# Later scalings of queries and keys, and one more tile for raw weights, in a two-layer decoder trunk

## The chip, the cores and the metric

The kernel runs on one core of one Trainium2 chip. The metric is the device time of one execution in microseconds (us), lower is better. The engines have short names here: PE is TensorE (matmuls), DVE is VectorE, ACT is ScalarE, POOL is GpSimd, and SP is SyncE, which here only issues DMA transfers. POOL also issues some.

## The reference

Two layers act on x of 512 tokens by 2048 features, all in float32. Layer 0 is forgetting attention (FoX) with 16 heads of 128, layer 1 multi-scale retention with 8 heads (queries and keys of 256, values of 512). Each mixer's output is multiplied by a SiLU gate before the output projection. What matters here, cut to its core:

```python
# layer 0
q, k, v, gate, f_logit = split(x @ fox_w_in)           # 2048 columns each, 16 for f_logit
q = rms_norm(q, q_gain); k = rms_norm(k, k_gain)       # per head: x * rsqrt(mean(x^2) + eps) * gain
c = cumsum(log_sigmoid(f_logit + b_f))
p = softmax(q @ k.T * 128**-0.5 + c_i - c_j, causal)
h = layer_norm(sqrt(2) * x + (p @ v * silu(gate)) @ fox_w_out)
# layer 1
q, k, v, gate = split(h @ ret_w_in)                    # 2048, 2048, 4096, 4096 columns
o = retention(rotary(q), rotary(k), v)                 # decay per head
out = layer_norm(sqrt(2) * h + (group_norm(o) * silu(gate)) @ ret_w_out)
```

`sqrt(2)` is `DEEPNORM_ALPHA` for a depth of 2.

## The kernel before

**Products.** Every float32 matrix is split into a high part (ACT copies it to a reduced float32, L340) and a low part (DVE subtracts the high part, L341); a product is three matmuls, high by high, low by high and high by low (`mm3`, L345 to L347). The projections are done in units. A unit multiplies a 2048 by 1024 (wide) or 2048 by 512 (narrow) slice of weights by a Strassen-Winograd scheme: seven products, called p1 to p7, instead of eight, with sums of quarters of the weights and of the activations. A product is cut into blocks: four in a wide unit, two in a narrow one. A wide block is twelve matmuls of 512 columns.

**Weights of a block.** A quarter of the weights comes by DMA on SP's queue into a raw tile, `w_raw` (L615); the first quarter goes into `w_q` (L606), a running sum. DVE adds a raw tile to `w_q` (L635) or two raw tiles to one another (L630), then ACT and DVE split the sum into `w_h` and `w_l`. There are three raw tiles, st0 to st2. `new_raw` takes the tile that has been free longest from a list called `stock`, and `end_raw` puts it back. The products p3 and p7 together need two raw tiles per block.

**Order of the work.** The order of all instructions is written out when the program is built, by a planner (class `Order`). Time is counted in slots, one for each block of matmuls. In a slot the planner first finishes the block before, adds weights three blocks ahead and splits two ahead, loads up to nine ahead as long as raw tiles are free, writes the block's matmuls, and then lets side tasks take steps. A side task is a generator: `yield need(dve=..., wait=n)` asks that n slots have passed since its last step, that named tiles are free, and that the work put on DVE (and on ACT) since does not exceed an allowance, 4.4 us for DVE, of which each slot works off 2.72. When a block needs a tile that is not free, the planner writes rounds of 2.7 us without matmuls until the tasks have freed it (`require`).

**Queries and keys of layer 0.** The heads are treated in eight pairs. A unit's sinks copy a pair's raw queries and keys into the tiles in0 and in1 (L1088) while ACT sums their squares (L1113). For every second pair (2 and 4) the copy is parked in DRAM and fetched later. The task `normed` then makes the reciprocal roots: DVE writes a first guess by integer arithmetic (L313 to L315), and three rounds of Newton's method follow. In pairs 6 and 7 (`quick`) DVE does these too; in pairs 0 to 5 POOL does, four small operations a round (L333 to L336, `iterate_aside`). After a wait in slots the four scalings follow on DVE (L1177), then PE transposes the scaled rows (L1209), and ACT and DVE split them by L1188 and L1190. With that in0 and in1 are free for the next pair, and the two heads of the pair, tasks of their own, can go on to scores, softmax and the product with the values.

**The last units.** Units 14 to 17 are the second output projection, all wide. Unit 16 adds the residual to the first half of the columns, and unit 17 to the second half, in the tiles g0, g2 and in0 with in1 (`add_z`, L1594, with the statistics for the layer norm at L1605). L517 and L525 finish the sums of products of a unit and free their PSUM banks. Meanwhile other forms of the activations are fetched (L949) and split for the second half of the units' sum.

**Lending.** The task `lend` takes a tile that has no user for some time, puts it into `stock` as one more raw tile, and takes it out again when a flag is set and the tile is back in `stock`. Before, it is used once, for the tile k0 in the first unit. Another such tile, `room`, is lent by `split_room` and given back by `join_room` when unit 16 begins.

Of the kernel before, what the change touches and what calls it, by code (L numbers as in the profile page):

```python
# [53 lines left out]
FIRST = (("p2",), ("p1",))  # L54
REST = (("p5",), ("p6",), ("p3", "p7"), ("p4",))
# [35 lines left out]
class Order:  # L91
# [21 lines left out]
    def give(self, ring, after=0):  # L113
        if after:
            self.later.append((self.now + after, ring))
        elif ring == "mmp" and not self.soon(self.due):

            self.emptied.append(self.due)
        else:
            self.free[ring] += 1  # L120
# [15 lines left out]
    def spawn(self, steps, rank=2):  # L136

        task = dict(steps=steps, last=self.now - 1, rank=rank)
        try:
            task["need"] = next(steps)  # L140
        except StopIteration:
            return
        at = sum(t["rank"] <= rank for t in self.tasks)
        self.tasks.insert(at, task)
# [103 lines left out]
def need(dve=0.0, act=0.0, pe=0.0, wait=1, until=lambda: True, **rings):  # L248
    return dict(dve=dve, act=act, pe=pe, wait=wait, until=until, rings=rings)
# [3 lines left out]
def trunk(ctx: ExitStack, tc: tile.TileContext, xq, x, fb_f, columns, wf_in, narrow, wide, ln_g, ln_b, rot, decay,  # L253
# [7 lines left out]
    spawn, take, give, free, require = o.spawn, o.take, o.give, o.free, o.require  # L261

    def f32(t):
        return t.bitcast(F32)

    def sb8(name, tag, dt=F32):
        return pool.tile([P, 4, 512], dt, name=name, tag=tag)
# [36 lines left out]
    def rsqrt(*args):  # L304
        for _ in rsqrt_steps(*args, steps=False):
            pass

    def rsqrt_steps(dst, src, n, scale, eps, aside=None, steps=True):

        h = pool.tile([P, n], F32, name="rsq_h", tag=f"rsq_h{n}")  # L310
        t = pool.tile([P, n], F32, name="rsq_t", tag=f"rsq_t{n}")

        nc.vector.tensor_scalar(h, src, 0.5 * scale, 0.5 * eps, op0=ALU.mult, op1=ALU.add)  # L313
        nc.vector.tensor_scalar(t.bitcast(I32), h.bitcast(I32), 1, None, op0=ALU.logical_shift_right)
        nc.vector.tensor_scalar(dst.bitcast(I32), t.bitcast(I32), -1.0, float(0x5EF759DF - 2 ** 31),  # L315
                                op0=ALU.mult, op1=ALU.add)
        if aside is not None:
            aside.append((h, t, dst))
            return
        for i in range(3):  # L320
            if i == 1 and steps:
                yield need(dve=1.2, wait=0)
            if n == 1:
                nc.vector.scalar_tensor_tensor(t, dst, h, dst, op0=ALU.mult, op1=ALU.mult)
            else:
                nc.vector.tensor_mul(t, dst, dst)
                nc.vector.tensor_mul(t, t, h)
            nc.vector.scalar_tensor_tensor(dst, t, 1.5, dst, op0=ALU.subtract, op1=ALU.mult)

    def iterate_aside(h, t, r):  # L330

        for _ in range(3):
            nc.gpsimd.tensor_mul(t, r, r)  # L333
            nc.gpsimd.tensor_mul(t, t, h)
            nc.gpsimd.tensor_scalar(t, t, -1.5, None, op0=ALU.add)
            nc.gpsimd.tensor_mul(r, r, t)  # L336
# [26 lines left out]
    stock, whose = ["st0", "st1", "st2"], {}  # L363
# [14 lines left out]
        take("y0")  # L378
        give("g2")

    def lend(tag):

        yield need(**{tag: 1})
        take(tag)
        stock.append(tag)
        give("st")
        yield need(until=lambda: fox.get("wide") and tag in stock and free["st"])
        stock.remove(tag)
        take("st")
        give(tag)  # L390
# [614 lines left out]
    fox = dict(heads=0, norms=0, emptied=0)  # L1005
# [62 lines left out]
    class Pair:  # L1068
# [13 lines left out]
        def take(self, m, n, tile, done):  # L1082
            def copy():
                yield need(act=0.5, until=self.has_room)
                if self.raw is None:
                    self.new_raw()
                    self.new_sums()
                nc.scalar.activation(self.raw[m][:, :, n * 256:(n + 1) * 256], tile, AF.Copy)  # L1088
                yield need(act=1.2)
                self.squares(m, n, tile, 0)  # L1090
                done()
                self.have += 1

            spawn(copy(), 0)
# [62 lines left out]
        def normed(self):  # L1157

            yield need(until=lambda: self.have == 4 and fox["norms"] == self.i)
            raw = [self.raw[s // 2][:, s % 2] for s in range(ST)]  # L1160
            r = self.ss
            flat = [r.rearrange("p a b -> p (a b)")] * 2
            if self.quick:
                yield need(dve=1.2)
                yield from rsqrt_steps(*flat, 4 * ST, 1.0 / P, QK_EPS)
            else:
                yield need(dve=0.6)
                guess = []
                rsqrt(*flat, 4 * ST, 1.0 / P, QK_EPS, guess)
                iterate_aside(*guess[0])  # L1170
                yield need(wait=2)
            scaled = {}
            for s in range(ST):
                yield need(dve=0.6, wait=0)
                scaled[s] = o.due
                v = raw[s].rearrange("p (h d) -> p h d", h=4)
                nc.vector.tensor_mul(v, v, r[:, s, :, None].to_broadcast([P, 4, P]))  # L1177
            yield need(until=lambda: all(free[t] for t in self.tags))
            for t in self.tags:
                take(t)  # L1180
            self.qk = sb8("qk_h", self.tags[0], F32R), sb8("qk_l", self.tags[1], F32R)

            def to_parts(t, s):

                parts = [(gain, t[:, i:i + 2], *(p[:, i:i + 2, s * P:(s + 1) * P] for p in self.qk))
                         for i, gain in ((0, gq), (2, gk))]
                for gain, x, h, _ in parts:
                    nc.scalar.activation(h, x, AF.Copy, scale=gain)  # L1188
                for gain, x, h, l in parts:
                    nc.vector.scalar_tensor_tensor(l, x, gain, f32(h), op0=ALU.mult, op1=ALU.subtract)  # L1190
                self.due = o.due
                give("mmp")

            t, s, last = {}, ST if self.quick else 0, None
            for q in range(ST if self.quick else 0):
                yield need(act=0.75, dve=0.7, pe=0.45, wait=1 - q % 2, mmp=1, until=lambda: o.soon(scaled[q]))
                t[q] = by4(mmp())
                for h in range(4):
                    nc.tensor.transpose(t[q][:, h], raw[q][:, h * P:(h + 1) * P], ident)
                to_parts(t[q], q)  # L1200
            can = lambda: s < ST and free["mmp"] and o.soon(scaled[s])
            while s < ST or last is not None:
                yield need(act=0.75, dve=0.7, pe=0.45, until=lambda: last is not None or can())
                new = None
                if can():
                    new = s
                    t[s] = by4(mmp())
                    for h in range(4):
                        nc.tensor.transpose(t[s][:, h], raw[s][:, h * P:(h + 1) * P], ident)  # L1209
                    s += 1  # L1210
                if last is not None:
                    to_parts(t[last], last)
                last = new
            give("in0")
            give("in1")
            fox["emptied"] = self.i + 1
            yield need()
            fox["norms"] = self.i + 1
# [232 lines left out]
    vg = [Unit(wide, g, gate_and_value(g), u2="k2") for g in range(4)]  # L1451
# [19 lines left out]
            else:  # L1471
                halves[i] = partial(split_x, *part)
    first.run(BOTH, halves=halves, then={len(BOTH) - 1: lambda: (spawn(forget()), core(0))}, before=before, ahead=ahead)
    vg[0].run(FIRST + REST, then={"p1": lambda: spawn(lend("k0")), "p7": lambda: fox.update(wide=True)})
    for i in (1, 3):
        both[i].run(then={"p4": lambda i=i: (core(i), spawn(pairs[i + 1].fetch()), core(i + 1))})
        vg[(i + 1) // 2].run()
# [44 lines left out]
    def two_banks():  # L1522
# [5 lines left out]
        BOTH, then={len(BOTH) // 2 - 1: lambda: spawn(fetch("a21", "k2", "k0", "k1")), len(BOTH) - 1: late})  # L1528
# [3 lines left out]
    st = {}  # L1532
# [182 lines left out]
    def last_banks():  # L1715
# [4 lines left out]
    sink, steps = add_z(0, ALPHA, x_rows, "plain", 2)  # L1720
    Plain(wide, 4, sink, last_banks).run(
        HELD, then={8: lambda s=steps: spawn(s(), 1)})
# [6 lines left out]
    sink, steps = add_z(1, ALPHA, x_rows, "each")  # L1729
# [256 lines left out]
    for h in heads[1:]:  # L1986
        if h.h == 2:
            spawn(biases())
        h.qk_unit.run(then={"p3": lambda h=h: spawn(h.attend())})
        then = fetch_while(1) if h.h == RH - 1 else {}  # L1990
        last = then.get("p4", lambda: None)
        h.vg_unit.run(SLOW if h.h == 1 else ORDER, leaves=h.h == RH - 1,
                      then={**then, "p4": lambda h=h, last=last: (spawn(h.retain()), last())})
# [106 lines left out]
    half = lambda s, c: z_res[s, c]  # L2100
    spawn(join_room(), 0)
    sink, steps = add_z(0, 1, half, "order")
    Unit(wide, 16, sink, u2="k2").run(then={0: lambda s=steps: spawn(s(), 1)})
    sink, steps = add_z(1, 1, half, "early")
    Unit(wide, 17, sink, u2="k2").run(EARLY, then={0: lambda s=steps: (spawn(s(), 1), spawn(biases_there(), 0)), "p2": lambda: spawn(last_gains(), 0),
                                          "p3": lambda: (spawn(first_stores(), 0), spawn(last_stores()))}, last=True)
# [53 lines left out]
```

## Time and profile before

| | us |
|---|---|
| median of 3 runs | 2323.4 |
| lowest and highest run | 2322.31, 2323.48 |
| the profiled execution | 2324.2 |
| its span, from the first to the last instruction | 2322.4 |

The profile is one execution, recorded by the hardware profiler. Its page gives busy times, a chain of waits, groups of instructions and DMA issues; the trace behind it can be asked for waits, for the instructions in order of time, and for sums over windows. A row of the timeline reads: start, duration, engine, line, operation, output <- inputs, shapes, count of merged instructions, and in brackets the idle time of the engine just before it and what ended that. A row of waits reads: engine, line and output that waited, what it waited for, and the total, the number and the longest of the waits. Matmuls are pipelined: a matmul's row lasts longer than the distance to the next start, so PE's speed is read from starts.

### The profile page before, as it was taken

The numbers are of one execution on the slowest core, as the hardware profiler recorded it, in microseconds if no ns is written. First come the engines' busy times: TensorE is split into PE (matmuls) and PEld (weight loads), VectorE is DVE, ScalarE is ACT, GpSimd is POOL, SyncE is SP. The second block draws the span as 40 slices with busy tenths as digits, with TensorE's granted clock in tenths as the row PEclk, the third lists the DMA queues.
The fourth block names the chain that finished last, engine by engine and source line by source line (L and its number), as shares of the span: only waits on it lengthen the run. The fifth ranks groups of instructions, "written<-read, shape, count | busy, mean of one in ns | idle before, by whom it ended". The sixth has DMA issues, their size and how long they took to land.

```text
span 2322.4 us, 32788 instructions
## 1 busy us (share of the span) xinstructions
PE 2288.3 (99%) x12381; PEld 1969.6 (85%) x12381; DVE 1869.8 (81%) x2375; ACT 1219.0 (52%) x1795; POOL 200.6 (9%) x323
## 2 busy tenths in 40 slices
PE   9999999999999999999999999999999999999996
PEld 9888788788899888889889898988888898788785
DVE  5886787787765666789989888888988889988888
ACT  4555656556555535664544445354545445555534
POOL 0100110111000000010101001010101001020001
PEclk9999999999999999999999999999999999999998
DMA  6465465454545467784675757575656658698767
GB/s 230 144 211 189 167 197 185 168 191 157 197 156 162 137 215 241 244 215 157 213 254 207 235 180 228 194 203 196 212 183 198 210 173 268 206 252 276 240 219 205
DMA packets 162687, 471.07 MB, mean 203 GB/s; under 512 B 17472, under 2 KB 34000, under 8 KB 162016
## 3 DMA queue, kind: packets, MB, share of 16 engines
q1 hardware_dynamic: 136464, 395.02, 50.1%
q0 software_dynamic: 26064, 73.95, 13.0%
q8 instruction: 97, 1.59, 0.3%
q14 instruction: 62, 0.51, 0.1%
HBM read 409.10 MB, written 64.00 MB: 204 GB/s over the span
## 4 chain that ended last, share of the span: by engine, by line
PE 85%; DVE 7%; ACT 3%; issue 2%; DMA 2%; POOL 1%; SPq 0%; DVEq 0%; ACTq 0%; POOLq 0%
PE acc L345 25%; PE acc L346 25%; PE acc L347 25%; DVE w_l L341 3%; PE mmp L345 2%; PE mmp L346 2%; PE mmp L347 2%; ACT w_h L340 2%; DVE w_q L635 2%; PE mmp L1390 1%; DMA w_raw<-in_wide 1%; PE mmp L1242 1%; DMA room<-in_wide 1%; PE mmp L1941 1%; PE mmp L1209 0%
## 5 line engine op out<-in xcount | busy, mean ns | idle before, releaser
L340 ACT ACTIVATE w_h<-w_q 128x1024 fp32r<-128x1024 f32 x360 | 380.9, 1059 | 436.8 <-DVE w_q L635 229.1
L345 PE MATMUL acc<-w_h,a 128*128 128x512 f32 (+1 forms) x1440 | 534.3, 371 | 3.3 <-DVE kept L525 2.5
L341 DVE TENSOR_TENSOR w_l<-w_raw,w_h 128x1024 fp32r<-128x1024 f32 (+1 forms) x311 | 379.2, 1219 | 189.3 <-ACT w_h L340 187.8
L346 PE MATMUL acc<-w_l,a 128*128 128x512 f32 (+1 forms) x1440 | 527.2, 366 | 1.9 <-DVE w_l L341 1.9
L340 ACT ACTIVATE w_h<-w_raw 128x1024 fp32r<-128x1024 f32 (+1 forms) x311 | 328.3, 1056 | 379.6 <-PE acc L347 186.7
L347 PE MATMUL acc<-w_h,a 128*128 128x512 f32 (+1 forms) x1440 | 527.5, 366 | 0.0
L341 DVE TENSOR_TENSOR w_l<-w_q,w_h 128x1024 fp32r<-128x1024 f32 x360 | 439.7, 1222 | 108.0 <-ACT w_h L340 101.0
L346 PE MATMUL acc<-w_l,s 128*128 128x512 f32 (+1 forms) x1280 | 487.3, 381 | 8.2 <-DVE w_l L341 8.2
L345 PE MATMUL acc<-w_h,s 128*128 128x512 f32 (+1 forms) x1280 | 491.9, 384 | 0.0
L347 PE MATMUL acc<-w_h,s 128*128 128x512 f32 (+1 forms) x1280 | 486.3, 380 | 0.0
L345 PEld LDWEIGHTS acc<-w_h,a 128*128 128x128 f32 x1440 | 271.7, 189 | 48.1 <-issue 5.9
L346 PEld LDWEIGHTS acc<-w_l,a 128*128 128x128 f32 x1440 | 271.9, 189 | 45.0 <-DVE w_l L341 4.0
L347 PEld LDWEIGHTS acc<-w_h,a 128*128 128x128 f32 x1440 | 271.5, 189 | 45.0
L346 PEld LDWEIGHTS acc<-w_l,s 128*128 128x128 f32 x1280 | 241.6, 189 | 55.3 <-DVE w_l L341 13.4
L347 PEld LDWEIGHTS acc<-w_h,s 128*128 128x128 f32 x1280 | 241.2, 188 | 46.1
L345 PEld LDWEIGHTS acc<-w_h,s 128*128 128x128 f32 x1280 | 241.3, 189 | 43.2 <-issue 0.9
L635 DVE TENSOR_TENSOR w_q<-w_q,w_raw 128x1024 f32<-128x1024 f32 x216 | 263.2, 1221 | 7.9 <-DMA w_raw<-in_wide 5.5
L345 PE MATMUL acc<-a,w_h 128*128 128x256 f32 x464 | 131.4, 283 | 0.0
L347 PE MATMUL acc<-a,w_l 128*128 128x256 f32 x464 | 131.3, 283 | 0.0
L346 PE MATMUL acc<-a,w_h 128*128 128x256 f32 x464 | 131.3, 283 | 0.0
L347 PE MATMUL acc<-s,w_l 128*128 128x256 f32 x448 | 126.8, 283 | 0.0
L346 PE MATMUL acc<-s,w_h 128*128 128x256 f32 x448 | 126.7, 283 | 0.0
(235 smaller groups left out, 2964.2 us busy)
## 6 DMA issues: line engine op xcount, KB each, us to landing
w_raw<-in_wide SPq DMA_DIRECT2D x362, 512.0 KB, 3.8
w_raw<-in_narrow SPq DMA_DIRECT2D x103, 512.0 KB, 3.9
w_q<-in_wide SPq DMA_DIRECT2D x72, 512.0 KB, 4.5
room<-in_wide SPq DMA_DIRECT2D x48, 512.0 KB, 4.5
y_s<-ny POOLq DMA_DIRECT2D x48, 256.0 KB, 7.3
y_s<-y POOLq DMA_DIRECT2D x40, 256.0 KB, 6.8
w_q<-in_narrow SPq DMA_DIRECT2D x18, 512.0 KB, 3.8
y_raw<-y_a SPq DMA_DIRECT2D x18, 512.0 KB, 5.6
```

What stands on the lines that cost most here:

```text
L340: nc.scalar.activation(h, src, AF.Copy)
L341: nc.vector.tensor_sub(l, src, f32(h))
L345: nc.tensor.matmul(ps, a[0], b[0], start=start, stop=False, skip_group_check=True)
L346: nc.tensor.matmul(ps, a[0], b[1], start=False, stop=False, skip_group_check=True)
L347: nc.tensor.matmul(ps, a[1], b[0], start=False, stop=stop, skip_group_check=True)
L635: nc.vector.tensor_add(u.chain[c], u.chain[c], t)
L1242: nc.tensor.transpose(tp[g][:, at], p[q][0][:, k * P:(k + 1) * P], ident)
L1390: nc.tensor.matmul(ps[:, k * P:], vh[:, k], pT[:, k, k * P:], start=k == 0, stop=k == ST - 1)
L1941: nc.tensor.transpose(ps[t - 1][:, i], g[t - 1][:, i * P:(i + 1) * P], ident)
```

## The change

Two edits. In `normed`, the wait between POOL's roots and the scalings becomes five slots instead of two, for pairs 0 to 5. And `lend` gets the name of the flag that ends the loan as an argument: the loan of k0 in the first unit keeps its flag `wide`, and in unit 16 the tile in1 is lent as a raw tile from the end of the first block, until the product p7 is finished and sets the flag `half`.

```diff
-    def lend(tag):
+    def lend(tag, over):
 
         yield need(**{tag: 1})
         take(tag)
         stock.append(tag)
         give("st")
-        yield need(until=lambda: fox.get("wide") and tag in stock and free["st"])
+        yield need(until=lambda: fox.get(over) and tag in stock and free["st"])
         stock.remove(tag)
         take("st")
         give(tag)
...
                 rsqrt(*flat, 4 * ST, 1.0 / P, QK_EPS, guess)
                 iterate_aside(*guess[0])
-                yield need(wait=2)
+                yield need(wait=5)
...
-    vg[0].run(FIRST + REST, then={"p1": lambda: spawn(lend("k0")), "p7": lambda: fox.update(wide=True)})
+    vg[0].run(FIRST + REST, then={"p1": lambda: spawn(lend("k0", "wide")), "p7": lambda: fox.update(wide=True)})
...
-    Unit(wide, 16, sink, u2="k2").run(then={0: lambda s=steps: spawn(s(), 1)})
+    Unit(wide, 16, sink, u2="k2").run(then={0: lambda s=steps: (spawn(s(), 1), spawn(lend("in1", "half"), 0)),
+                                            "p7": lambda: fox.update(half=True)})
```

## The prediction

> **What bounds the kernel now.** First the page: its span, its busy times and the one row of landing times that I need.
>
> ```profile
> span 2322.4 us, 32788 instructions
> PE 2288.3 (99%) x12381; PEld 1969.6 (85%) x12381; DVE 1869.8 (81%) x2375; ACT 1219.0 (52%) x1795; POOL 200.6 (9%) x323
> w_raw<-in_wide SPq DMA_DIRECT2D x362, 512.0 KB, 3.8
> ```
>
> PE bounds nearly everything, so an edit pays only where PE stands still. Second, the waits: PE's two longest entries, and VectorE (DVE) on GpSimd (POOL).
>
> ```profile
> PE acc L346 <- DVE w_l L341: 10.1, 11, 2.7
> PE acc L345 <- DVE kept L525: 2.5, 4, 1.1
> DVE qk_raw L1177 <- POOL rms_ss L336: 6.1, 4, 2.0
> ```
>
> Each row gives the total, the number and the longest wait. PE idles 10.1 us for the low parts of split weights, which DVE makes at L341. Third, the timeline where this is longest: PE, DVE and POOL as the queries and keys of pair 1 are normed.
>
> ```profile
> 252.62 0.39 PE L347 MATMUL acc<-w_h,s 128*128 128x512 f32 x1
> 252.84 0.39 PE L345 MATMUL acc<-w_h,s 128*128 128x512 f32 x1
> 255.93 0.80 PE L346 MATMUL acc<-w_l,s 128*128 128x512 f32 x1 [2.70 <-DVE w_l L341]
> 256.52 0.63 PE L347 MATMUL acc<-w_h,s 128*128 128x512 f32 x1
> 256.95 0.63 PE L345 MATMUL acc<-w_h,s 128*128 128x512 f32 x1
> ...
> 243.92 0.18 DVE L315 TENSOR_SCALAR rms_ss<-rsq_t 128x16 int32<-128x16 int32 x1
> ...
> 246.06 2.38 DVE L635 TENSOR_TENSOR w_q<-w_q,w_raw 128x1024 f32<-128x1024 f32 x2
> 248.48 1.23 DVE L341 TENSOR_TENSOR w_l<-w_q,w_h 128x1024 fp32r<-128x1024 f32 x1
> 251.71 1.90 DVE L1177 TENSOR_TENSOR qk_raw<-qk_raw,rms_ss 128x512 f32<-128x512 f32 x3 [2.01 <-POOL rms_ss L336]
> 253.52 1.22 DVE L635 TENSOR_TENSOR w_q<-w_q,w_raw 128x1024 f32<-128x1024 f32 x1
> 254.66 1.22 DVE L341 TENSOR_TENSOR w_l<-w_q,w_h 128x1024 fp32r<-128x1024 f32 x1
> ...
> 257.53 1.22 DVE L341 TENSOR_TENSOR w_l<-w_q,w_h 128x1024 fp32r<-128x1024 f32 x1
> ...
> 244.87 1.27 POOL L335 TENSOR_SCALAR rsq_t<-rsq_t 128x16 f32<-128x16 f32 x1
> 246.23 1.14 POOL L336 TENSOR_TENSOR rms_ss<-rms_ss,rsq_t 128x16 f32<-128x16 f32 x1
> 247.45 1.08 POOL L333 TENSOR_TENSOR rsq_t<-rms_ss 128x16 f32<-128x16 f32 x1
> 248.60 1.18 POOL L334 TENSOR_TENSOR rsq_t<-rsq_t,rsq_h 128x16 f32<-128x16 f32 x1
> 249.87 0.25 POOL L335 TENSOR_SCALAR rsq_t<-rsq_t 128x16 f32<-128x16 f32 x1
> ...
> 251.46 0.22 POOL L336 TENSOR_TENSOR rms_ss<-rms_ss,rsq_t 128x16 f32<-128x16 f32 x1
> ```
>
> DVE leaves a first guess of the roots (L315), POOL improves it in twelve small operations, and two blocks later DVE scales with the result (L1177). The roots are late: DVE idles 2.01 us, then does three scalings before the next weight. POOL's operations take 0.22 us alone and 1.08 to 1.27 us beside DVE's additions and subtractions. Normal matmul starts are 0.22 us apart; here they are 3.09, so PE loses **2.86 us**. Pair 3 repeats this:
>
> ```profile
> 437.56 0.39 PE L345 MATMUL acc<-w_h,s 128*128 128x512 f32 x1
> 440.65 0.50 PE L346 MATMUL acc<-w_l,s 128*128 128x512 f32 x1 [2.70 <-DVE w_l L341]
> ```
>
> Last, unit 16, the last but one: PE, DVE, and the load for which DVE waits.
>
> ```profile
> 2197.87 0.39 PE L345 MATMUL acc<-w_h,s 128*128 128x512 f32 x1
> 2199.66 0.50 PE L346 MATMUL acc<-w_l,s 128*128 128x512 f32 x1 [1.41 <-DVE w_l L341]
> ...
> 2207.51 0.39 PE L347 MATMUL acc<-w_h,a 128*128 128x512 f32 x1
> 2209.02 0.47 PE L345 MATMUL acc<-w_h,a 128*128 128x512 f32 x1 [1.12 <-DVE kept L525]
> ...
> 2193.52 1.22 DVE L341 TENSOR_TENSOR w_l<-w_raw,w_h 128x1024 fp32r<-128x1024 f32 x1
> 2197.25 1.23 DVE L630 TENSOR_TENSOR w_raw<-w_raw 128x1024 f32<-128x1024 f32 x1 [2.51 <-DMA w_raw<-in_wide]
> ...
> 2207.06 0.69 DVE L1605 BATCH_NORM_STATS2 ln_st<-z 128x6 f32<-128x512 f32 x1
> 2207.67 1.20 DVE L525 TENSOR_TENSOR kept<-kept,acc 128x1024 f32<-128x1024 f32 x1
> ...
> DVE w_raw L630 <- DMA w_raw<-in_wide: 5.8, 3, 2.5
> 2187.69 5.13 SPq L615 DMA_DIRECT2D w_raw<-in_wide  x2
> ```
>
> **Part one: two blocks become five.** No operation is added or removed. The four scalings of pairs 0 to 5 come three blocks later in the written order. On DVE they pass three blocks' additions and splits; behind them follow, as late, PE's transposes, ScalarE's (ACT's) splits, the fetches of pairs 2 and 4 and the heads' loads on SP, and the heads' stores on POOL. No engine gets a new wait.
>
> A block is twelve matmuls at 0.226 us, so 2.71 us. Without the wait and the scalings, the addition L635 starts at 249.71 and, by the starts at 253.52 and 254.66 (1.14 apart), L341 ends at 249.71 + 1.14 + 1.22 = 252.07. PE wants it at 253.07: 1.0 us to spare instead of 2.86 missing. In the following blocks DVE has an addition and a subtraction, 2.28 us of 2.71, and gains 0.43 us each. At the fifth block, about 257.8 (251.71 − 2.01 + 3 × 2.71), it is some 2.3 us ahead. Three scalings cost 3 × 0.60 = 1.8 us and fit. The stalls of pairs 1 and 3 go: 2 × 2.86 = **5.72 us**. Bounds: nothing of it (the scalings stall there too) to all; I take all less a remainder, below.
>
> Are the roots there? Four operations had been slowed by 249.7; eight remain. Two per block run beside DVE's two long ones and one in the 0.43 us gap: 8 / 3 × 2.71 = 7.2 us, done at 256.9, 0.9 us early. If DVE leaves no gap, eight take 8 × 1.17 (mean of the four slow rows) = 9.4 us, done at 259.1: DVE would wait 1.3 us, and with 1.8 of scalings exceed its 2.3 of lead by 0.8. Per pair, twice, that is 0 to 1.6 us; I charge **0.5**, nearer the case with gaps, since the rows of 249.87 on show POOL quick as soon as DVE pauses.
>
> The Trainium skill, "SBUF — State Buffer", section "Who interferes with whom", speaks against the edit: a DVE instruction with two SBUF inputs and a GpSimd instruction that reads SBUF exclude one another for a whole instruction. The slow rows agree. By it, DVE no longer pausing also keeps POOL slower; that is the first rival.
>
> After the first stall matmuls start 0.43 us apart. The windows give the clock (seventh figure on):
>
> ```profile
> 252.00:260.00 8.00, 5.30 (x18) 3.95 (x17) 8.00 (x10) 3.03 (x3) 0.00 (x0) 0.79 0.37 122
> ```
>
> A clock of 0.79 over 8 us is 3.4 us at half speed, 1.7 us lost. Without it PE would want the next weight at 255.93 + 11 × 0.226 = 258.4, and L341 from 257.53 ends at 258.75, so 0.35 is lost anyway: **1.4 us**, between 0 and 1.7. It should go with the stall.
>
> The Trainium skill, "TensorE: Matmul & The Clock Gate", section "What's actually happening", halves the clock after an idle window of about 3.4 us, free-running. Here 2.86 us sufficed once and not at pair 3; by the rule alone the dip was not the stall's, and the sum would be 1.4 us less, 2315.6.
>
> What becomes late? Pair 4's last transposes must leave in0 and in1 before pair 5's queries are copied in:
>
> ```profile
> L1209 PE MATMUL mmp<-ident,qk_raw x16: 272/273/328, 499.7 to 527.1; 128*128 128x128 f32 x16
> L1088 ACT ACTIVATE qk_raw<-kept x3: 613/616/621, 538.2 to 551.7; 128x512 f32<-128x512 f32 x3
> 578.91 1.01 ACT L469 ACTIVATE kept<-acc 128x1024 f32<-128x1024 f32 x1
> ```
>
> The gap is 11 us. Pairs 3 and 4 follow one another, so the delay is 3 blocks (8.1 us) to 6 (16.3): copies come up to 5 us late. The tiles they empty are next written at 578.91, 27 us after the last of these copies. Cost 0, hidden by that room.
>
> **Part two: in1 lent in unit 16.** A fourth tile for raw weights; no instruction is added on a compute engine. The SP row holds two issues, the first at 2187.69, the second 0.33 long and ending at 2192.82, so issued at 2192.49. The addition L630 of 2197.25 waits for the second; it took 4.8 us to be usable (median landing 3.8). Each load follows the end of a subtraction L341, which frees its tile. With four tiles a load goes one release earlier: this one at 2187.69, usable at about 2192.5, before DVE first wants it (2197.25 − 2.51 = 2194.74). The 2.51 us go; were only part of those 4.8 us gained, part of them. In1's earlier users belong to unit 14, so SP does not stand on it, nor the loads behind: those for the next forms and the residual. PE's 1.79 − 0.22 = **1.57 us** goes; bounds 0 to 1.57. In1 must be back before unit 17 adds its first half; no raw tile is asked for once unit 16's are loaded, so it is: cost 0, and if not, PE would stand in unit 17. The second gap of 1.51 − 0.23 = 1.28 us arises because DVE, never idle since 2197.25, reaches L525 2.6 us after p7's last matmul (one block, 2.71 us, before 2207.51). With DVE 2.5 us earlier about **1.0 us** goes; bounds 0 to 1.28.
>
> Sum: 5.72 + 1.4 − 0.5 + 1.57 + 1.0 = **9.2 us**. The profiled execution took 2324.2 us (span and 1.8 around it) and would take 2315.0. The runs shown have a median 0.8 lower, so I predict **2314.2**.
>
> **Rivals.**
> 1. The moved scalings find no lead, or late roots. For: POOL's margin of 0.9 us is thin. Against: DVE gains 0.43 us per block. Pairs 1 and 3 give back 1.6 instead of 0.5 (2315.3); if pairs 2 and 4, which had no such stall, also pay a full 1.8, 2318.9.
> 2. The lent tile brings nothing, because landing, not the release, is late. For: 4.8 us against a median of 3.8. Against: the issue follows a release. 2314.2 + 2.6 = 2316.8.
> 3. Slower: the handover of in0 and in1 from pair 4 to 5. The order is written with PE standing still in rounds of 2.7 us when a tile is not free. It decides once copies come over 27 us late; four rounds, 10.8 us, then exceed the gain: 2314.2 + 10.8 = 2325.0. Against: at most 5 us are in sight.
> 4. The edit of part one does not move what matters, because DVE's allowance had already put the scalings late. Only 2.6 us come: 2320.8. Against: three scalings stand two blocks after the guess.
>
> **How the numbers follow.** Forecast 0.60; rivals 0.17, 0.10, 0.07 (slower) and 0.06. Up to 0.2% (4.6 us, about what a measurement can tell) counts as no change, so the border is 2318.8. Forecast, rival 2 and 0.10 of rival 1 lie below it: 0.80; the rest of rival 1 and rival 4: 0.13; slower 0.07. The low end takes every upper bound: 5.72 + 1.7 + 1.57 + 1.28 = 10.3, 2313.1, less the runs' spread of 1.2 and what pairs 2 and 4 may gain of DVE's other waits for POOL, 6.1 − 2 × 2.01 us: 2311. The high end is rival 1's worst plus the spread: 2320.
>
> **What would show it.** Right: no PE gap over 1 us beside L1177, no row of DVE waiting for L336, clock 1.0 there, no wait of L630 over 1 us in unit 16, and L525 no longer holding PE there. Wrong: new gaps before L346 three blocks later, DVE still waiting for POOL, L630 still waiting for loads, or PE idle for L1088.

## The result, and the profile after

| | us |
|---|---|
| kernel before, median of its 6 runs | 2323.6 |
| changed kernel, median of 6 runs | 2313.61 |
| lowest and highest run | 2310.58, 2315.74 |
| the profiled execution, its span | 2313.67, 2311.9 |
| ratio to before, 95% interval | 0.9958, 0.9944 to 0.9971 |

The change took 10 us off, 0.42%, and the forecast was 2314.2. Five of the six runs before lie between 2322.31 and 2323.95 us; the sixth took 3510.94, a time that no other run of any kernel here came near, and the ratio leaves it out. A second set of five runs of the changed kernel had a median of 2311.63 us and a ratio of 0.9957 (0.9944 to 0.9969). From the page of the changed kernel and PE's waits in it, the rows that matter here:

```profile
span 2311.9 us, 32799 instructions
PE 2284.2 (99%) x12381; PEld 1969.0 (85%) x12381; DVE 1871.4 (81%) x2375; ACT 1217.9 (53%) x1795; POOL 213.0 (9%) x323
```

```profile
PE acc L346 <- DVE w_l L341: 2.8, 7, 0.7
PE mmp L1209 <- ACT o L1397: 1.4, 2, 0.7
PE mmp L1242 <- DVE kept L985: 1.3, 1, 1.3
PE mmp L345 <- DVE sm L1293: 0.9, 1, 0.9
PE acc L345 <- DVE kept L525: 0.8, 3, 0.3
```

PE did the same 12381 matmuls. Its waits for low parts of weights fell from 10.1 to 2.8 us, those for L525 from 2.5 to 0.8. Three entries are new; more on them below. POOL was busy 12.4 us longer with the same 323 instructions.

The same stretch at pair 1, first DVE, then POOL, then the window that had the slow clock:

```profile
243.66 0.17 DVE L315 TENSOR_SCALAR rms_ss<-rsq_t 128x16 int32<-128x16 int32 x1
244.53 1.23 DVE L341 TENSOR_TENSOR w_l<-w_q,w_h 128x1024 fp32r<-128x1024 f32 x1 [0.70 <-ACT w_h L340]
...
255.12 1.22 DVE L341 TENSOR_TENSOR w_l<-w_q,w_h 128x1024 fp32r<-128x1024 f32 x1
256.45 1.90 DVE L1177 TENSOR_TENSOR qk_raw<-qk_raw,rms_ss 128x512 f32<-128x512 f32 x3
258.26 1.22 DVE L341 TENSOR_TENSOR w_l<-w_q,w_h 128x1024 fp32r<-128x1024 f32 x1
```

```profile
244.29 0.22 POOL L334 TENSOR_TENSOR rsq_t<-rsq_t,rsq_h 128x16 f32<-128x16 f32 x1
244.60 1.27 POOL L335 TENSOR_SCALAR rsq_t<-rsq_t 128x16 f32<-128x16 f32 x1
...
249.60 1.10 POOL L335 TENSOR_SCALAR rsq_t<-rsq_t 128x16 f32<-128x16 f32 x1
...
255.39 1.02 POOL L336 TENSOR_TENSOR rms_ss<-rms_ss,rsq_t 128x16 f32<-128x16 f32 x1
```

```profile
252.00:260.00 8.00, 8.00 (x37) 6.64 (x36) 7.89 (x9) 4.14 (x5) 4.17 (x4) 1.00 0.61 196
```

PE is busy for all of the 8 us (5.30 before) and the clock is 1.00 (0.79 before). DVE no longer waits for POOL. But POOL's roots end at 255.39 + 1.02 = 256.41, and the scalings start at 256.45: the room is 0.04 us. Ten of POOL's twelve operations took more than 1 us; before, four did.

Where the time went can be summed from the distances between PE's matmul starts: a distance over the usual one for its size (0.227 us at 512 columns, 0.120 at 256, 0.109 at 128) is lost time. This table is worked out from the starts of the two traces. Starts of L1390, the product with the values, are left out: they are farther apart than these, by the same 14.4 us in all in both traces. So are differences of 0.03 us and less.

| stretch of the span | lost before | lost after |
|---|---|---|
| pair 1 (240 to 262 us) | 4.5 | 0.0 |
| pair 3 (420 to 460) | 3.3 | 0.4 |
| unit 16 (2135 to 2215) | 4.1 | 0.8 |
| 262 to 420, heads of pairs 1 and 2 | 3.0 | 5.0 |
| 460 to 700, heads of pairs 3 to 5 | 4.3 | 3.8 |
| all others | 22.5 | 21.6 |
| sum | 41.7 | 31.5 |

No term of the forecast speaks of the row "all others"; half of its 0.9 us lies near 1186 us, of which more at the end.

PE's new gaps in the changed kernel, each longer than half a microsecond:

```profile
162.60 0.38 PE L345 MATMUL mmp<-qk_h 128*128 128x256 f32 x1 [0.91 <-DVE sm L1293]
...
328.61 0.65 PE L1242 MATMUL mmp<-ident,p 128*128 128x128 f32 x4 [1.31 <-DVE kept L985]
329.95 0.66 PE L1209 MATMUL mmp<-ident,qk_raw 128*128 128x128 f32 x4 [0.69 <-ACT o L1397]
...
511.39 0.66 PE L1209 MATMUL mmp<-ident,qk_raw 128*128 128x128 f32 x4 [0.69 <-ACT o L1397]
```

They are the side tasks themselves, scores and transposes of attention, which now meet other work in their slots. In unit 16 the timeline has these waits of DVE and PE, and the waits summed over the unit this row:

```profile
2180.77 1.23 DVE L630 TENSOR_TENSOR w_raw<-w_raw 128x1024 f32<-128x1024 f32 x1 [0.84 <-DMA w_raw<-in_wide]
2185.65 1.23 DVE L630 TENSOR_TENSOR w_raw<-w_raw 128x1024 f32<-128x1024 f32 x1 [0.25 <-DMA w_raw<-in_wide]
...
2163.49 0.50 PE L346 MATMUL acc<-w_l,s 128*128 128x512 f32 x1 [0.30 <-DVE w_l L341]
```

```profile
DVE w_raw L630 <- DMA w_raw<-in_wide: 1.1, 2, 0.8
```

L630 waits 1.1 us in all instead of 5.8. The gap before L346 near 2199 and the one before L345 near 2209 have gone; one of 0.30 us is left.

### The profile page after: what moved, and what is told of

It is laid out like the page before. It is cut to its first block, busy times and chain, and to the rows that moved or that the text cites. A ratio compares the mean times of both kernels' runs of the same rounds, so it can differ in the third digit from the quotient of the medians.

```text
span 2311.9 us, 32799 instructions
## 1 busy us (share of the span) xinstructions
PE 2284.2 (99%) x12381; PEld 1969.0 (85%) x12381; DVE 1871.4 (81%) x2375; ACT 1217.9 (53%) x1795; POOL 213.0 (9%) x323
## 4 chain that ended last, share of the span: by engine, by line
PE 88%; DVE 5%; DMA 2%; ACT 2%; issue 1%; SPq 0%; DVEq 0%; ACTq 0%
PE acc L345 26%; PE acc L346 26%; PE acc L347 26%; DVE w_l L341 2%; PE mmp L345 2%; PE mmp L346 2%; PE mmp L347 2%; PE mmp L1390 1%; DVE w_q L635 1%; ACT w_h L340 1%; PE mmp L1242 1%; DMA room<-in_wide 1%; PE mmp L1941 1%; DMA w_raw<-in_wide 1%; DMA z_in<-z_res 0%
## 5 line engine op out<-in xcount | busy, mean ns | idle before, releaser
L345 PE MATMUL acc<-w_h,a 128*128 128x512 f32 (+1 forms) x1440 | 533.8, 371 | 1.8 <-DVE kept L525 0.8
L346 PE MATMUL acc<-w_l,a 128*128 128x512 f32 (+1 forms) x1440 | 527.2, 366 | 1.5 <-DVE w_l L341 1.5
L345 PE MATMUL acc<-w_h,s 128*128 128x512 f32 (+1 forms) x1280 | 491.3, 384 | 0.0
L346 PE MATMUL acc<-w_l,s 128*128 128x512 f32 (+1 forms) x1280 | 485.8, 380 | 1.3 <-DVE w_l L341 1.3
L345 PEld LDWEIGHTS acc<-w_h,a 128*128 128x128 f32 x1440 | 271.7, 189 | 46.4 <-issue 3.9
L346 PEld LDWEIGHTS acc<-w_l,a 128*128 128x128 f32 x1440 | 271.9, 189 | 44.6 <-DVE w_l L341 3.2
L346 PEld LDWEIGHTS acc<-w_l,s 128*128 128x128 f32 x1280 | 241.1, 188 | 46.4 <-DVE w_l L341 4.1
L345 PEld LDWEIGHTS acc<-w_h,s 128*128 128x128 f32 x1280 | 241.0, 188 | 43.2 <-issue 0.9
L345 PE MATMUL acc<-a,w_h 128*128 128x256 f32 x464 | 131.4, 283 | 0.0
L346 PE MATMUL acc<-a,w_h 128*128 128x256 f32 x464 | 131.3, 283 | 0.0
L346 PE MATMUL acc<-s,w_h 128*128 128x256 f32 x448 | 126.7, 283 | 0.0
```

Source lines behind the costliest of these rows:

```text
L345: nc.tensor.matmul(ps, a[0], b[0], start=start, stop=False, skip_group_check=True)
L346: nc.tensor.matmul(ps, a[0], b[1], start=False, stop=False, skip_group_check=True)
```

## The experiments

The theory is that PE lost time at pairs 1 and 3 because DVE stood waiting for late roots and then had three scalings to do with too little lead, and in unit 16 because a raw tile came free too late for its load. The rivals: the scalings alone make the stall; POOL needs a fixed 7.5 us, as it ran before; the loads land late whatever tile they have; the handover of in0 and in1 limits how late the scalings may come.

**Each part alone.** Part one without the loan, as an edit of the kernel before:

```diff
-                yield need(wait=2)
+                yield need(wait=5)
```

> Part one alone: five blocks, nothing lent. If the two parts act apart, the gaps of 2.86 us at pairs 1 and 3 and the slow clock go, those of 1.57 and 1.28 us in unit 16 stay: about 7 us less than the kernel before. If the fourth tile brings nothing of its own, the whole 10 us come.

Measured 2315.98 us, ratio 0.9969 (0.9957 to 0.998): 7.2 us less than the 2323.2 of the kernel before beside it. In unit 16 of this run:

```profile
DVE w_raw L630 <- DMA w_raw<-in_wide: 5.2, 3, 2.1
PE acc L346 <- DVE w_l L341: 1.2, 2, 0.9
PE acc L345 <- DVE kept L525: 1.1, 1, 1.1
```

The loan alone, as an edit of the changed kernel:

```diff
-                yield need(wait=5)
+                yield need(wait=2)
```

> Part two alone: in1 is lent, two blocks stay. If the fourth tile takes away the wait for weights: no wait of L630 over 1 us in unit 16, PE gives back 2.5 to 3.3 us there, the gaps at pairs 1 and 3 stay, about 3 us less than before. If landing and not the tile is late: no difference.

Measured 2320.0 us, ratio 0.9984 (0.9975 to 0.9993): 3.2 us less. The parts act apart: 7.2 + 3.2 = 10.4, and both together gave 10.0 and, in the second set, 11.2. The waits of unit 16 are those of the changed kernel (L630: 1.1 us). The gaps at pairs 1 and 3 are as before, and so is the slow clock, at the first and not at the second, as the windows around them show (the second figure is PE's busy time, the one after POOL's the clock):

```profile
252.00:260.00 8.00, 5.32 (x20) 4.01 (x19) 8.00 (x9) 3.48 (x4) 0.00 (x0) 0.79 0.36 131
436.00:444.00 8.00, 5.32 (x25) 4.07 (x25) 8.00 (x10) 3.04 (x3) 0.00 (x0) 1.00 0.37 125
```

**The roots left out.** The kernel before without POOL's three rounds; the scalings take the first guess:

```diff
                 rsqrt(*flat, 4 * ST, 1.0 / P, QK_EPS, guess)
-                iterate_aside(*guess[0])
                 yield need(wait=2)
```

> The kernel before, without POOL's three rounds on the roots (the scalings use the first guess, so the output is not the reference's). Two blocks stay. If POOL's lateness is most of the stall and three scalings on a DVE with little lead the rest, DVE never waits, and PE gaps of about 0.85 us stay at pairs 1 and 3: about 4 us less, more without the slow clock. If the three scalings alone make the stall, gaps of 2.9 us stay. If POOL's lateness is all, the gaps go entirely: about 7 us less.

Measured 2317.13 us, ratio 0.9975 (0.9966 to 0.9984), 6.1 us less: more than the 4 expected for the stalls alone, as the slow clock at pair 1 went too. DVE and PE at pair 1, and PE at pair 3 (lines behind the edit have numbers one lower):

```profile
248.84 1.89 DVE L1176 TENSOR_TENSOR qk_raw<-qk_raw,rms_ss 128x512 f32<-128x512 f32 x3
...
253.06 0.50 PE L346 MATMUL acc<-w_l,s 128*128 128x512 f32 x1 [0.60 <-DVE w_l L341]
...
434.29 0.50 PE L346 MATMUL acc<-w_l,s 128*128 128x512 f32 x1 [0.59 <-DVE w_l L341]
```

By starts (252.06 to 253.06, less 0.23) the gap is 0.77 us, and 0.75 at pair 3, against 2.86. So about 2.1 us of each stall was POOL's lateness and 0.8 the scalings', which falls between the two rivals as the prediction's sum had it. By that sum DVE's lead before the scalings, the time by which it is ahead of PE, was 1.8 − 0.77 = 1.0 us.

**Three and four blocks.** Both parts; for pairs 1 and 3 four blocks, for the other pairs two:

```diff
-                yield need(wait=5)
+                yield need(wait=4 if self.i in (1, 3) else 2)
```

> Both parts, four blocks for pairs 1 and 3, two for the others. From the runs so far: without POOL's work and at two blocks the gap is 0.77, so DVE's lead before the three scalings is 1.81 - 0.77 = 1.04 us there, and 0.43 more for each later block; POOL's twelve operations need 12.8 us beside a DVE that does not pause. Gap = 1.81 + DVE's wait for POOL - lead. At four blocks DVE waits about 0.75, its lead is 1.9: gaps of about 0.7 us at pairs 1 and 3, 1 to 1.5 us more than with five for these pairs (2313.2). If two blocks were short of POOL's 7.5 us only (as it ran before), four are ample and nothing changes (2311.9).

Measured 2315.41 us, ratio 0.9964 (0.9952 to 0.9977). The place itself is as the sum had it: DVE waits 0.76 us and the gap is 0.78 (257.58, not shown, to 258.59, less 0.23).

```profile
254.37 1.90 DVE L1177 TENSOR_TENSOR qk_raw<-qk_raw,rms_ss 128x512 f32<-128x512 f32 x3 [0.76 <-POOL rms_ss L336]
...
258.59 0.50 PE L346 MATMUL acc<-w_l,s 128*128 128x512 f32 x1 [0.62 <-DVE w_l L341]
```

The time is 2 us more than expected; 1.6 us of that is a gap before L1242 near 388, where the side tasks met other work again. And with three blocks for pairs 1 and 3:

```diff
-                yield need(wait=5)
+                yield need(wait=3 if self.i in (1, 3) else 2)
```

> The same with three blocks for pairs 1 and 3. By the same sum DVE waits about 1.2 us and leads by 1.5: gaps of about 1.5 us, some 3 us more than with five for these pairs (2314.9). If POOL needs 7.5 us whatever DVE does, three blocks (8 us and more) are enough and nothing changes (2311.9).

Measured 2318.47 us, ratio 0.9981 (0.9972 to 0.999), 3.6 us more than the 2314.9 expected.

```profile
252.88 1.90 DVE L1177 TENSOR_TENSOR qk_raw<-qk_raw,rms_ss 128x512 f32<-128x512 f32 x3 [1.36 <-POOL rms_ss L336]
...
257.10 0.50 PE L346 MATMUL acc<-w_l,s 128*128 128x512 f32 x1 [1.62 <-DVE w_l L341]
```

DVE waits 1.36 us and the gap is 1.78, at pair 3 as well, where 1.2 and 1.5 were expected. That explains 0.6 of the 3.6 us; in the trace, 2.4 us more than with five blocks for these pairs are lost among the heads between 262 and 700 us. With two, three, four and five blocks the gap is 2.86, 1.78, 0.78 and 0. A fixed 7.5 us of POOL is out: after three blocks it would have been ready. By the sum of wait, scalings and lead, DVE's lead is 1.0, 1.4 and 1.8 us at two, three and four blocks, some 0.4 more for each block, as the prediction had it. Five is the fewest that leaves no gap.

**Five blocks only where the roots were late.**

```diff
-                yield need(wait=5)
+                yield need(wait=5 if self.i in (1, 3) else 2)
```

> Both parts, but five blocks for pairs 1 and 3 only, two for pairs 0, 2, 4 and 5. If the new gaps of the changed kernel (about 1.1, 1.5 and twice 0.85 us, near 161, 327, 329 and 510 us) come from the delay in the other pairs, they go and some small ones of before (0.4 to 0.5 us each) come back: 1 to 2 us less than the changed kernel. If they come from the delay in pairs 1 and 3 itself, handed down the chain of pairs, they stay: no difference.

Measured 2311.89 us, ratio 0.9955 (0.9942 to 0.9967): 1.7 us under the changed kernel's first median, though the intervals overlap. The trace tells the new gaps apart: those that ended at 162.60 and 328.61 (1.07 and 1.47 us by starts) are gone, so they came from the delay in pairs 0 and 2, the only ones of the four that run by then; those before L1209, 0.85 us near 328 and 510, stay, so they come from pairs 1 and 3; and a third one appears at pair 5:

```profile
PE mmp L1209 <- ACT o L1397: 2.1, 3, 0.7
...
579.84 0.65 PE L1209 MATMUL mmp<-ident,qk_raw 128*128 128x128 f32 x4 [0.75 <-ACT o L1397]
```

With five blocks for pair 5 too:

```diff
-                yield need(wait=5)
+                yield need(wait=5 if self.i in (1, 3, 5) else 2)
```

> Both parts, five blocks for pairs 1, 3 and 5, two for 0, 2 and 4. Pair 5's roots are not late at two blocks, so DVE's scalings gain nothing there; only the gap of 0.9 us near 579, which appeared with five blocks for pairs 1 and 3 alone, can move: 0 to 1 us less than that kernel (2311 to 2312).

Measured 2310.75 us, ratio 0.9945 (0.9933 to 0.9958), the lowest median of all; the gap that ended at 579.84 is gone. Beside the changed kernel, once more:

> The changed kernel once more, beside the next one on the same chip, to compare the two. By the gaps of their profiles (new gaps of about 1.1 and 1.5 us gone in the next one) it should be 2 to 3 us slower than the next; if the difference seen so far was between chips, they are equal.

> Both parts, five blocks for pairs 1, 3 and 5 only, once more: 2 to 3 us less than the changed kernel; if the difference seen so far was between chips, they are equal.

Measured 2311.63 us (2311.12 to 2314.72) for the changed kernel and 2311.54 (2309.45 to 2312.09) for the other, not 2 to 3 us apart, ratios 0.9957 (0.9944 to 0.9969) and 0.9949 (0.9935 to 0.9963). The profiled executions stand 3 us apart, 2314.72 and 2311.61, the medians do not. That the second is faster than the changed kernel isn't shown.

**A fifth tile.** With in0 lent beside in1, on the kernel with five blocks for pairs 1 and 3:

```diff
-... spawn(lend("in1", "half"), 0)),
+... spawn(lend("in1", "half"), 0), spawn(lend("in0", "half"), 0)),
```

> As the kernel with five blocks for pairs 1 and 3, with in0 lent beside in1 in unit 16: five raw tiles. If the fourth tile already hides the loads, nothing changes (within 0.5 us of 2311.9), and L630 waits no less. If loads are still late, the rest of unit 16's gaps (0.75 us) go too.

Measured 2313.59 us, ratio 0.9955 (0.9941 to 0.9968). L630's wait in unit 16 goes to nothing, but PE's loss there is 0.7 us against 0.8 with one tile: one tile is enough. The median is 1.7 us higher than without, where a rise of at most 0.5 was expected; its trace has 2.6 us in one gap near 1188, told of below.

**How late may the scalings come?** Both parts, eight blocks for pairs 0 to 5:

```diff
-                yield need(wait=5)
+                yield need(wait=8)
```

> Both parts, eight blocks for pairs 0 to 5. Rival 3 of the prediction put the point where the handover of in0 and in1 costs time at copies 27 us late. Against the kernel before, pairs 3 and 4 are delayed by six blocks each, 32.6 us in a row, against 11 us of room: copies of pair 5 about 21 us late, so PE never waits for them. No cost by that; small gaps as in the changed kernel: 2312 to 2316.

Measured 2311.65 us, ratio 0.9952 (0.9936 to 0.9969), a shade under the 2312 to 2316 expected: no slower than five. And twelve:

```diff
-                yield need(wait=5)
+                yield need(wait=12)
```

> Both parts, twelve blocks for pairs 0 to 5. Ten blocks each for pairs 3 and 4, 54 us in a row, less 11 us of room: copies of pair 5 some 43 us late, past the 27 us. If the point was placed rightly, PE stands still by 10 us or more near pair 5's copies: 2324 or more. If the chain has other room (pair 4 waits for pair 3's heads anyway), it stays at 2312 to 2317.

Measured 2319.9 us, ratio 0.9987 (0.9977 to 0.9996), between the two times that were expected. First pair 4's transposes and pair 5's copies in this run (durations, then first and last start), with ACT's last reading of the copied tiles and its next write of such a tile; then PE's longest gaps, then the window around the second:

```profile
L1209 PE MATMUL mmp<-ident,qk_raw x16: 270/272/273, 544.6 to 557.2; 128*128 128x128 f32 x16
L1088 ACT ACTIVATE qk_raw<-kept x3: 627/630/631, 558.8 to 559.8; 128x512 f32<-128x512 f32 x3
...
566.21 0.18 ACT L1113 ACTIVATION_READ_ACCUMULATOR kept<-kept 128x1 f32 x1
566.45 1.03 ACT L469 ACTIVATE kept<-acc 128x1024 f32<-128x1024 f32 x1
```

```profile
686.79 0.55 PE L1242 MATMUL mmp<-ident,p 128*128 128x128 f32 x3 [1.69 <-ACT pT L1265]
710.25 0.63 PE L1199 MATMUL mmp<-ident,qk_raw 128*128 128x128 f32 x4 [1.93 <-DVE qk_l L1190]
```

```profile
707.00:715.00 8.00, 6.07 (x40) 5.86 (x39) 3.57 (x6) 2.62 (x5) 0.04 (x1) 0.79 0.01 2
```

The copies come right behind the last transposes, so they do wait for in0 and in1. The first starts 20.6 us later than in the kernel before (538.2), in a kernel that is ahead by then: measured by the units' matmuls started so far, the first is 30 us late and the last of the three 17, not the 43 expected. The room behind them is about used up, as L469, the next write of such a tile, comes 0.06 us after ACT's last reading, but PE does not wait there. Most of the lost time lies 125 us later, where the delayed heads of pair 5 run into pair 6 and PE goes from one side task to the next without blocks between. The kernel still ends below the one before.

## Why the prediction was right, step by step

The time, the direction and the two mechanisms were right. By the table of lost time, pair 1 gave 4.5 us where 2.86 + 1.4 were forecast, pair 3 2.9 (2.86), unit 16 3.3 (2.57), the late roots cost 0 (0.5), the heads cost 1.4 (0), and all others gave 0.9 (0): 10.2 against 9.2. The single terms:

- **Stalls at pairs 1 and 3, 5.72 us.** All of it came. The runs with two to five blocks, and the one without roots, show both halves of the reason: late roots, and too little lead for the scalings. Rival 4 is out: the scalings moved from 251.71 to 256.45.
- **The charge of 0.5 us for late roots.** It was 0 there, but by a hair. The prediction took DVE to leave a gap of 0.43 us in each block. It left none: it worked on without pause from 244.53 on and was done earlier, so the scalings came at 12.8 us after the guess, not 13.9, and the roots at 12.75, not 13.0. Both estimates erred, and the margin of 0.9 us was 0.04. That the roots' time came out so near is luck. The prediction counted eight operations left at 249.7, but of the twelve two short operations (at 244.28 and 244.56) and four long ones are done by then in its trace, and six are left. By its rule of three to a block six would have been done at 255.1. They kept their long time of over 1 us each to the end, 6.8 us from 249.60 on, and the two errors all but cancel. The rule of the Trainium skill that was cited ("SBUF — State Buffer", "Who interferes with whom") agrees with the trace: POOL's operations took 1.02 to 1.27 us, one beside each of DVE's, until the end, and POOL's busy time rose by 12.4 us.
- **The slow clock, 1.4 us.** It went: 4.5 us were lost at pair 1 and 2.86 of these were the gap, so it was worth some 1.6. The loan alone kept the gap and the slow clock with it. The sum with 1.4 us less, by the rule of the Trainium skill ("TensorE: Matmul & The Clock Gate", "What's actually happening") taken alone, was the worse one.
- **Unit 16, 1.57 + 1.0 us.** The loss fell from 4.1 to 0.8, by 3.3; the term was 0.7 us short, as it took 1.0 of the second gap's 1.28 and counted none of the small ones. The loan alone measured 3.2. That the release of a tile and not the landing was late (rival 2) is settled: a fourth tile took the wait from 5.8 to 1.1 us, and a fifth from there to none, while loads issued between 2150 and 2200 us landed in 4.7 us at the median before and in 4.3 after.
- **What becomes late, 0 us.** Here the prediction lacked a term. The handover from pair 4 to 5 cost PE nothing, as said, though 1.6 us of its room were left (531.4 to 533.0 in the changed kernel):

```profile
L1209 PE MATMUL mmp<-ident,qk_raw x16: 272/273/328, 511.4 to 531.4; 128*128 128x128 f32 x16
L1088 ACT ACTIVATE qk_raw<-kept x3: 615/625/627, 533.0 to 543.5; 128x512 f32<-128x512 f32 x3
```

  But the heads and transposes that follow in a new place brought four gaps of 0.85 to 1.47 us, the first of them before 262 us, and took away three of 0.53: about 1.4 us more between 262 and 700. The 0.5 charged elsewhere, the 0.7 missing in unit 16 and the 0.9 of all others, which no term forecast, hid this in the sum. So that the first median came within 0.6 us of the forecast is in part luck; that of the second set is 2.6 below it.
- **Rival 3, the slower one.** It was far off: five blocks used 9 of the 11 us of room, and eight no more of PE's time. Even twelve blocks only just reach the point that the prediction named, so what lies beyond it wasn't tried; but the first price shows elsewhere, in the heads of pairs 5 and 6, and the kernel is still not slower than before.
- **The range.** Its low end, 2311, does not follow from what the prediction takes off: 2313.1 − 1.2 − 2.1 is 2309.8. The lowest of the eleven runs of the changed kernel took 2310.58.

## What to carry to other kernels

When one engine's small jobs must finish before another engine's next step, count how long they take while that other engine does not pause, not how long they took while it stood waiting: here 12.4 us against 7.4, from POOL's first operation to the end of its last. A gap is then the wait plus the inserted work less the lead, and moving the step by a block changes each of these by an amount that the trace before already shows. A tile lent as one more buffer was worth the wait for its release and no more; a second one brought nothing. And where an order is written by a planner, expect a move to cost or save a microsecond or two in tasks that follow it, and delay only the steps that need it.

## What the runs showed of the hardware

**The clock.** In four of the fourteen traces the clock went to half once before the kernel's end, each time for 3.41 us. From the clock records, with the time since full speed began at the start of the kernel:

```
kernel before        slow for 3.41 us, after  249.17 us =  73 x 3.4133
the loan alone       slow for 3.41 us, after  249.17 us =  73 x 3.4133
without the roots    slow for 3.41 us, after 2184.53 us = 640 x 3.4133
twelve blocks        slow for 3.41 us, after  706.56 us = 207 x 3.4133
```

All begin on a fixed grid of 3.4133 us. The Trainium skill, "TensorE: Matmul & The Clock Gate", section "What's actually happening", gives such a free-running window and asks for one idle window. Here less was enough: without the roots PE idled 2.11 us in unit 16, and the clock fell to half for the window after:

```profile
2191.42 0.50 PE L346 MATMUL acc<-w_l,s 128*128 128x512 f32 x1 [2.11 <-DVE w_l L341]
```

```profile
2188.00:2196.00 8.00, 5.89 (x19) 4.39 (x18) 6.99 (x7) 2.12 (x3) 0.00 (x0) 0.79 0.40 132
```

The idle time of pair 3, 2.70 us, twice had no such effect. On the grid it falls into two windows, with 1.9 us in the first, while that of pair 1 has 2.3 us in one. Laid over the grid, PE's idle time by the rows of all fourteen traces agrees: the windows just before the four at half clock have 2.29, 2.25, 2.11 and 1.93 us of it, and no other window before the kernel's end has more than 1.89, not even where PE waits for 2.41 us near 1188 (0.9 in one window and 1.5 in the next). So it is the idle share of one window that fits, not the length of the wait, with the limit between 1.89 and 1.93 of 3.41 us here. It wasn't tested by itself.

**The spread.** Executions of one kernel, side by side, mostly differ by 1.6 to 6.6 us. A part of this lies near 1186 us, where DVE's order is the same in these kernels: PE waits there for L525, in the two profiled executions of the changed kernel for 0.31 and 0.95 us, with eight blocks for 1.54, and with two tiles lent for 2.41.

```profile
1186.84 0.47 PE L345 MATMUL acc<-w_h,a 128*128 128x512 f32 x1 [0.31 <-DVE kept L525]
```

```profile
1187.25 0.47 PE L345 MATMUL acc<-w_h,a 128*128 128x512 f32 x1 [0.95 <-DVE kept L525]
```

```profile
1186.05 0.47 PE L345 MATMUL acc<-w_h,a 128*128 128x512 f32 x1 [1.54 <-DVE kept L525]
```

```profile
1188.19 0.47 PE L345 MATMUL acc<-w_h,a 128*128 128x512 f32 x1 [2.41 <-DVE kept L525]
```

What makes it vary stays open. One trace of each kernel can therefore tell a gap's place, but not a median's last 2 us.
